# Summing expert rows at a token's rank in its group, and ending the layer group by group over gathered rows

## The chip, the cores and the metric

One core of one Trainium2 chip runs the whole program. The metric is device time in microseconds for one execution of one layer, the median of several runs. The engines are TensorE (PE in the rows, its weight load PEld), VectorE (DVE), ScalarE (ACT), GpSimd (POOL) and SyncE (SP). SP issues nearly all plain transfers in the order of its program; POOL issues those whose rows are picked by a table of indices.

## What is computed

512 tokens of 1024 features, with 16 learned tokens ahead of them, go through an attention branch and a state-space branch, which are merged and added to the input. The result `h` then goes through a mixture of experts and a last norm:

```
g_idx = argmax(v @ w_group + b_group)              # one of 4 groups
top_vals, top_idx = top_k(e_logits[g_idx], 2)      # two of the group's 8 experts
w = softmax(top_vals) * p_group[g_idx]
h = h + sum over the two experts e:  w_e * (silu(v @ gate_e) * (v @ up_e)) @ down_e
out = rmsnorm(h, norm_final)                       # v = rmsnorm(h, norm_ffn)
```

A token meets experts of one group alone. Run on its inputs, the reference's router puts 111, 155, 156 and 90 of the 512 tokens into groups 0 to 3, and no expert has more than 54 tokens.

## The kernel before

The input projections, the state-space branch and the attention come first (to about 480 us). Then `out_half` adds the merged branches to the input in `h2` (four blocks of 128 tokens on the partitions). `turn` stores each block's rows in DRAM as `vd`, and `norm_v` stores a factor behind each row. `choose`, `rank`, `find_slots` and `place` build tables with small products on TensorE and small operations on VectorE: every expert has 64 slots, experts 2p and 2p + 1 share the 128 partitions of pair p, and `idx[:, p]` and `tokf[:, p]` hold the token of each slot. `overflow` (on POOL) holds the weights of choices without a slot; a branch that runs only then is skipped here.

The expert stage runs over 16 pairs p, four of one group after another. Of a pair:

- `gather(p)` fetches the rows of the pair's tokens from `vd` into one of three buffers `xgs`, three pairs ahead, from POOL.
- `turn_x` transposes them on TensorE (`pxT`), and VectorE writes `xT`.
- `expert_gu` multiplies with the gate and up weights (`gu`), and ACT and DVE form the product `hp`.
- `expert_h` transposes that (`phT`, `hT`), `y_mm` multiplies with the down weights (`y`), and `y_split` weighs the result and splits it into two parts, `yh` on ACT and `yl` on DVE.
- `combine` adds the rows to their tokens: `st` is a matrix with a one where a slot's token number equals the column, and for each of the 4 blocks of 128 tokens and each half hh of the features two products (`yh`, `yl`) go to PSUM; DVE adds them to `h2`.

```
            for n, x in enumerate((yh_, yl_)):
                pe.matmul(pc, st[:, b * 128:(b + 1) * 128], x[:, c], start=(n == 0 and not on),
```

So a pair has 4 blocks x 2 halves x 2 parts = 16 such products. From pair 13 on (`HB`) the sums of blocks 2 and 3 stay in PSUM, which begins with eight products of `h2` with the identity (`sum_start`).

The weights stream through a ring of 6 places for gate and up weights (2 MB an expert, loaded by halves of the features, `load_gu`) and 7 for down weights (1 MB, `load_dn`). SP issues the loads of experts 2p + 6 and 2p + 7 when `expert_gu(p)` has read its places. A block `in_order` fixes the order of the named engines' instructions; elsewhere the framework's scheduler places them, also ahead of what stands earlier in the program. The last part takes the four blocks through squares, `rstd`, `scale` and a plain store of each half.

Of the kernel before, what the change touches and what calls it, by code (L numbers as in the profile page):

```python
# [9 lines left out]
F32 = mybir.dt.float32  # L10
# [9 lines left out]
T = 512  # L20
# [27 lines left out]
CAP = 64  # L48

# [10 lines left out]
for _n, _w in (("ident", 128), ("tri", 128), ("mask_s", 128), ("ones", 128),  # L60
               ("before", 128), ("ic", 104)):
    CST[_n] = (_o, _o + _w)
    _o += _w
# [8 lines left out]
def hybrid_layer(ctx: ExitStack, tc, A, out):  # L72
# [20 lines left out]
    def in_order(*engines):  # L93
        """the block's instructions run on these engines in the order of the program"""
# [51 lines left out]
    # blocks of 128 positions; block 0 starts with the meta tokens, block 4 has the last 16 positions  # L146
# [80 lines left out]
    def split_w(src, name, k, eng=dve):  # L227
        """two parts of [128, k, 1024 / k]"""
# [44 lines left out]
    def rms_feat(srcs, rngs, n, tag, nf=(0, 0)):  # L273
        """1/rms over features (partitions and list entries), broadcast over partitions"""
# [94 lines left out]
    p_misc = first[0]  # L369
# [40 lines left out]
    # dt = softplus(dt_raw + bias), token-major: column block 0 holds x chunks 0..3, block 4 the meta tokens  # L410
# [13 lines left out]
    # softplus(v) = max(v, 0) + log1p(exp(-|v|)), log1p(e) = 2 atanh(e / (2 + e))  # L424
# [13 lines left out]
    # a = dt * A;  cumulative sums within each chunk  # L438
# [14 lines left out]
    # decay[s, h] = exp(acs_last - acs_s)  # L453
# [46 lines left out]
    def gate_z(j):  # L500
        """2 silu(z)"""
# [24 lines left out]
    def ssd_a(c):  # L526
        """what a chunk needs besides the state before it"""
        n = NM if c == 4 else 128
        t0 = 0 if c == 4 else NM + c * 128
        # token-major x * dt, and times the decay to the chunk's end; B token-major, each group twice  # L530
# [3 lines left out]
        if c != 4:  # L534
            # decays between positions of the chunk: exp(acs_l - acs_s) where l >= s (elsewhere C B^T is masked)
# [127 lines left out]
    def branch_mms(pb_, wname, j, kk, oh, ol, last, parts="hl"):  # L663
        """the products of some k, first those of the weights' leading part"""
# [24 lines left out]
    # key blocks of 128 positions (block 4: 16); columns of the x queries that see each block  # L689
# [23 lines left out]
    # rows of q', k': 64 without position, 32 rotated, one that carries -max  # L713
# [13 lines left out]
    def load_wq(*which):  # L727
        """quarters of the query weights, (c, i0, i1) of each chunk c, loaded whole; what stays free of the tile"""
# [9 lines left out]
    def q_weights(c, i):  # L738
        """quarter i of chunk c of the query weights, [128, 2, 256] in two parts"""
# [9 lines left out]
    def rope(n):  # L749
        """rotated parts of the queries of heads 4 g4 .. 4 g4 + 3, in two steps"""  # L750
# [24 lines left out]
    def prep(j):  # L775
        """q' and k' of heads 2j, 2j + 1"""
# [24 lines left out]
    def find_max(h):  # L801
        """max over the keys each query sees"""
# [18 lines left out]
    def put_max(h):  # L821
        """-max into row 96 of q'"""
# [7 lines left out]
    def probs(h, h1=None):  # L830
        """exp(score - max), keys x queries, by key blocks"""
# [29 lines left out]
    def p_times_v(j, PP, eng=pool, mid=None):  # L861
        """heads 2j and 2j + 1 side by side on the array"""
# [8 lines left out]
        # the blocks' sum, for the rows' sums  # L871
# [7 lines left out]
    def row_sums(PP):  # L879
        """the rows' sums, each on 64 partitions"""  # L880
# [5 lines left out]
    def spread_sums(j, pl):  # L886
        """the sums over all partitions, 8 on each"""
# [8 lines left out]
    def invert(j, l8):  # L896
        """their inverses, each row's on 64 partitions again"""
# [46 lines left out]
    wq2[1], rotw[1] = q_weights(0, 1), q_weights(1, 1)  # L944
    PP, pos, l8s, lis = {}, {}, {}, {}
# [68 lines left out]
    # which pool holds each place of the ring, and how many of its kind lie there  # L1014
# [3 lines left out]
    def load_gu(e, parts=(0, 1)):  # L1018
        """by halves of the features"""
# [31 lines left out]
    wrt = rx.tile([128, T], F32, tag="rx", name="wrt")  # L1051
# [5 lines left out]
    # by halves of the tokens: [128, 2 blocks, 2 column tiles, 128 tokens] for two column tiles  # L1057
# [58 lines left out]
    # rows of h2 in DRAM, each with half of 1 / rms behind it  # L1116
    vd = drp.tile([T, D + 1], F32, name="vd")
# [3 lines left out]
    io32, io64, tok1 = ic[:, 4:36], ic[:, 36:100], ic[:, 100:104]  # L1121
    g_ffn = pv[:, PV["g_ffn"][0]:PV["g_ffn"][1]]
    # v @ w = (h2 @ (2 g * w)) * 1 / (2 rms(h2))
# [64 lines left out]
    def choose(b0, b1):  # L1188
# [62 lines left out]
        for b in range(nb):  # L1251
            oh12s.append(oh12[:, b])
# [522 lines left out]
```

## Time and profile before

| what | us |
|---|---|
| median of 3 runs (lowest to highest) | 850.42 (849.38 to 851.21) |
| the profiled execution: span of its instructions | 848.1 |
| what lies around the span, against the median | 2.3 |

The span runs from the first to the last instruction of the profiled execution. Times in the rows below count from its start. A row of the timeline gives start, duration, engine, line, operation and tiles, and in brackets how long the engine was idle and what ended the wait. "SPq" is SyncE's queue as it issues a transfer; the time to landing runs from the issue until all parts of the transfer have arrived.

### The profile page before, as it was taken

Reading aid. Unit: us, or ns where it says so; the run is one execution under the profiler, and the core shown is the slowest. Engines: PE = TensorE matmul, PEld = TensorE weight load, DVE = VectorE, ACT = ScalarE, POOL = GpSimd, SP = SyncE. Lnnn points to the kernel's source line nnn. Section 1 sums busy time; section 2 is a strip of 40 time slices with the busy share of each in tenths; the row PEclk is TensorE's granted clock in tenths of the full one; section 3 lists DMA queues with packets and bytes.
Section 4 is the critical chain, followed back from the end, with each engine's and each line's share of the span. In section 5 each row is a group of like instructions: output and inputs, shape, how many; then the busy total and the mean of one; then the engine's idle time right before and its main releaser. Section 6 shows DMA issues by size and latency. Waiting matters only on the chain.

```text
span 848.1 us, 11613 instructions
## 1 busy us (share of the span) xinstructions
PE 806.3 (95%) x4330; PEld 553.2 (65%) x4330; DVE 491.0 (58%) x1081; ACT 277.5 (33%) x525; POOL 133.5 (16%) x176
## 2 busy tenths in 40 slices
PE   4999999999999999999999999977999999999995
PEld 3999886777788778767665788863444444444452
DVE  4697439965357535666866654272546556556334
ACT  6445334333235552454643333210111111111114
POOL 5000104322011000024345000032000000000002
PEclk9999999999999999999999999987999999999998
DMA  7321235325212241112122955878999999999402
GB/s 246 107 90 62 100 111 163 125 85 165 75 63 100 72 164 60 35 32 61 36 74 53 388 219 213 298 276 206 419 417 420 419 418 419 418 419 412 173 1 99
DMA packets 40367, 163.53 MB, mean 193 GB/s; under 512 B 8640, under 2 KB 13008, under 8 KB 24176
## 3 DMA queue, kind: packets, MB, share of 16 engines
q1 hardware_dynamic: 36656, 156.68, 49.2%
q0 software_dynamic: 2832, 5.84, 2.3%
q8 instruction: 36, 0.59, 0.3%
q10 hardware_dynamic: 816, 0.20, 0.1%
q14 instruction: 27, 0.22, 0.1%
HBM read 159.43 MB, written 4.26 MB: 193 GB/s over the span
## 4 chain that ended last, share of the span: by engine, by line
PE 86%; DVE 5%; DMA 4%; ACT 2%; issue 1%; POOL 1%; SPq 0%; DVEq 0%; POOLq 0%; ACTq 0%
PE gu L1480 13%; PE y L1513 7%; PE pc L1542 6%; PE pbr L667 3%; PE pbr L670 3%; PE pbr L668 3%; PE po L870 2%; PE pxT L1452 2%; PE ga L240 2%; PE gs L240 2%; PE gs L241 2%; PE ga L242 2%; PE ga L241 2%; PE gs L242 2%; PE pout L1087 2%; PE pout L1089 2%
## 5 line engine op out<-in xcount | busy, mean ns | idle before, releaser
L1480 PE MATMUL gu<-gu,xT 128*64 128x512 f32 (+1 forms) x544 | 115.0, 576 | 0.0
L1480 PEld LDWEIGHTS gu<-gu,xT 128*64 128x64 f32 x544 | 37.9, 138 | 69.1 <-issue 65.5
L1545 DVE TENSOR_TENSOR h<-h,pc 128x512 f32<-128x512 f32 x108 | 66.8, 678 | 0.0
L1484 DVE SCALAR_TENSOR_TENSOR hp<-th,gu 128x256 f32<-128x256 f32 (+1 forms) x17 | 6.9, 405 | 100.0 <-ACT th L1483 100.0
L1513 PE MATMUL y<-dn,hT 128*64 128x512 f32 x256 | 58.7, 599 | 0.5 <-ACT hT L1496 0.5
L1483 ACT ACTIVATE th<-gu,rsl 128x256 f32<-128x256 f32 (+1 forms) x17 | 7.8, 461 | 149.9 <-PE gu L1480 149.9
L1542 PE MATMUL pc<-yh,st 128*128 128x512 f32 x110 | 47.3, 430 | 0.3
L816 DVE CUSTOM_DVE_ANT_0 sp<-sp,amask 128x144 f32<-128x144 f32 (+4 forms) x80 | 33.9, 459 | 18.0 <-PE sp L808 16.0
L1379 POOL DMA_INDIRECT xg<-vd,idx x16 | 16.0, 1002 | 178.4 <-PE pc L1542 161.8
L1542 PE MATMUL pc<-yl,st 128*128 128x512 f32 x110 | 43.2, 393 | 0.0
L1513 PEld LDWEIGHTS y<-dn,hT 128*64 128x64 f32 x256 | 16.9, 136 | 33.1 <-issue 26.9
L1520 ACT ACTIVATE yh<-y,wsl 128x512 fp32r<-128x512 f32 x30 | 20.6, 688 | 50.6 <-PE y L1513 50.6
L1521 DVE SCALAR_TENSOR_TENSOR yl<-y,wsl,yh 128x512 fp32r<-128x512 f32 x30 | 22.5, 751 | 20.7 <-ACT yh L1520 20.1
L1542 PEld LDWEIGHTS pc<-yh,st 128*128 128x128 f32 x110 | 20.7, 188 | 16.9 <-issue 11.4
L846 PE MATMUL st<-qs,kq 97*128 97x512 f32 (+4 forms) x80 | 28.7, 358 | 1.0 <-DVE kq L791 1.0
L1452 PEld LDWEIGHTS pxT<-cst,xg 128*128 128x128 f32 x128 | 14.4, 146 | 17.8 <-issue 17.8
L1454 DVE TENSOR_TENSOR xT<-pxT,pv 128x512 f32<-128x512 f32 x32 | 20.6, 682 | 6.6 <-PE pxT L1452 6.5
L847 PE MATMUL st<-qs,kq 97*128 97x512 f32 (+4 forms) x80 | 23.7, 296 | 0.2 <-DMA qs<-rs 0.2
L1452 PE MATMUL pxT<-cst,xg 128*128 128x128 f32 x128 | 18.3, 289 | 5.6 <-DMA xg<-vd,idx 5.6
L386 DVE SCALAR_TENSOR_TENSOR cacc<-xp,cwh,cacc 128x528 f32<-128x528 f32 x30 | 22.9, 762 | 0.4
L855 ACT ACTIVATE pw<-st 128x512 f32<-128x512 f32 (+1 forms) x32 | 16.7, 546 | 19.7 <-PE st L851 18.6
L848 PE MATMUL st<-qs,kq 97*128 97x512 f32 (+4 forms) x80 | 22.9, 294 | 0.0
(918 smaller groups left out, 2092.1 us busy)
## 6 DMA issues: line engine op xcount, KB each, us to landing
gu<-in_moe_gu_dram SPq DMA_DIRECT2D x64, 1024.0 KB, 14.7
dn<-in_moe_dn_dram SPq DMA_DIRECT2D x30, 1024.0 KB, 13.3
win<-in_win_dram SPq DMA_DIRECT2D x19, 1024.0 KB, 4.7
lm<-acd SPq DMA_DIRECT2D x16, 256.0 KB, 3.6
wbs<-in_wbs_dram SPq DMA_DIRECT2D x4, 1024.0 KB, 4.8
wba<-in_wba_dram SPq DMA_DIRECT2D x4, 1024.0 KB, 11.8
wo<-in_wout_dram SPq DMA_DIRECT2D x4, 1024.0 KB
ce<-acd SPq DMA_DIRECT2D x16, 128.0 KB, 7.3
```

Source lines behind the costliest of these rows:

```text
L240: pe.matmul(dst, ah, bh, start=(i == 0), stop=False)
L241: pe.matmul(dst, ah, bl, start=False, stop=False)
L242: pe.matmul(dst, al, bh, start=False, stop=(i == n - 1))
L667: pe.matmul(pb_, wh[:, k], oh[k], start=(k == 0), stop=False)
L668: pe.matmul(pb_, wh[:, k], ol[k], start=False, stop=False)
L816: dve.tensor_tensor_reduce(s_, s_, amask[:, L - nk + n0:L - nk + n1], 1.0, -3.0e38, op0=ALU.add, op1=ALU.max, accum_out=mx[:, n_:n_ + 1])
L846: pe.matmul(d_, kh_[0:97, kb], qh_[0:97, q0:q1], start=True, stop=False)
L1452: pe.transpose(pt[:, k * 128:(k + 1) * 128], xgs[p % NX][:, (hh * 4 + k) * 128:(hh * 4 + k + 1) * 128], ident)
L1480: pe.matmul(gu[f][r, :2 * n], xT[p][:, k, r], w, start=(k == 0), stop=(k == KD - 1), skip_group_check=True)
L1513: pe.matmul(yp[hh][e * 64:(e + 1) * 64], hT_[p][:, f, e * 64:(e + 1) * 64], dns[(2 * p + e) % ND][:, f, hh * 512:(hh + 1) * 512], start=(f ...
L1542: pe.matmul(pc, st[:, b * 128:(b + 1) * 128], x[:, c], start=(n == 0 and not on), stop=(n == 1 and (p == 15 or not kept and p < 15 - hh)), ...
L1545: dve.tensor_add(h2[:, b, c], h2[:, b, c], pc)
```

## The change

The sums of a group grow in PSUM over its four pairs, at a row that is the token's rank among its group's tokens (0 to 255, so two blocks of 128 rows and not four). `rank` now counts the 4 groups beside the 32 experts (36 columns, `ohc`), `place` puts the rank (`lpos`) beside the weight, and `y_start` compares with the rank. `group_tables`, `group_places` and `group_lists` turn the ranks into lists of tokens in pair 0. `group_rows(g)` gathers the group's rows of `h2` from `vd` into `res` in the group's third pair; `add`, `norm` and `scale` end the layer for the group in the pair behind its last, and `put_rows` scatters the finished rows to the output. `sum_start`, the 108 additions to `h2` and the last part over four blocks are gone. `vd` has 512 more rows, which begin as a copy of the input `x` and which are read only where the skipped branch has run.

The core of the diff (cut lines are marked "..."; line breaks and names as in the code):

```diff
+    vd = drp.tile([2 * T, D + 1], F32, name="vd")
+    nc.sync.dma_start(vd[T:, :D], A["x"])
+    nc.sync.dma_start(vd[T:, D:], A["x"][:, :1])
     PP, pos, l8s, lis = {}, {}, {}, {}
...
         dve.tensor_tensor(pen, bc(ic[:, None, 0:4], 4), bc(gf, 4), op=ALU.not_equal)
+        pool.tensor_scalar(ohc[:, b0:b1, 32:], pen, -1.0, 1.0, op0=ALU.mult, op1=ALU.add)
...
-                pe.matmul(rk[:, b * 32:(b + 1) * 32], trib if b2 == b else onesb, oh12s[b2],
+                pe.matmul(rk[:, b * 36:(b + 1) * 36], trib if b2 == b else onesb, oh12s[b2],
                           start=(b2 == 0), stop=(b2 == b), skip_group_check=True)
+        act.activation(rkg[:, b0:b1], ranks(b0, b1)[:, :, 32:], AF.Copy)
+        for k in range(2):
+            pool.tensor_tensor(vw[:, :, k, 1].rearrange("p b (g e) -> p b g e", g=4),
+                               ak[:, :, k].rearrange("p b (g e) -> p b g e", g=4),
+                               rkg[:, b0:b1, :, None].to_broadcast([128, b1 - b0, 4, 8]), op=ALU.mult)
...
     def overflow(b0):
+        pool.tensor_tensor(g4_, ohc[:, b0:b1, 32:], rkg[:, b0:b1], op=ALU.mult)
+        pool.tensor_tensor(g4_[:, :, :2], g4_[:, :, :2], g4_[:, :, 2:], op=ALU.add)
+        pool.tensor_tensor(gk[:, b0:b1], g4_[:, :, 0], g4_[:, :, 1], op=ALU.add)
         pool.tensor_scalar(wx, rkk, CAP - 0.5, None, op0=ALU.is_gt)
+        pool.tensor_scalar(g4_[:, :, 2], gk[:, b0:b1], GCAP - 0.5, None, op0=ALU.is_gt)
+        pool.tensor_tensor(wx, wx, g4_[:, :, 2:3].to_broadcast([128, b1 - b0, 2]), op=ALU.add)
+        pool.tensor_scalar(wx, wx, 0.5, None, op0=ALU.is_gt)
...
+    fin = btile("fin", n=T, tag="v").rearrange("p k n -> p (k n)")
+    res, gfin = [fin[:, b * (D + 1):(b + 1) * (D + 1)] for b in range(2)], fin[:, 2 * D + 2:3 * D + 2]
...
+        for x in res:
+            pool.memset(x, 0.0)
...
+    nc.sync.dma_start(gfin, bcast_row(A["g_fin"], D))
+
+    def put_rows(places, rows):
+        nc.gpsimd.indirect_dma_start(out=out, out_offset=bass.IndirectOffsetOnAxis(ap=places, axis=0),
+                                     in_=rows, in_offset=None, bounds_check=T - 1, oob_is_err=False)
...
-            if p == HB[0] and kh:
-                sum_start(HB[1])
...
-        dve.tensor_scalar(st, iot, tokf[:, p:p + 1], None, op0=ALU.is_equal)
+        dve.tensor_scalar(st, iot, lpos[:, p:p + 1], None, op0=ALU.is_equal)
...
-    def combine(p, hh, blocks=range(4)):
+    def combine(p, hh, blocks=range(2)):
         st, yh_, yl_ = y_[p]
...
+            if p % 4 == 0:
+                sums[b, hh] = ps("pc")
             for n, x in enumerate((yh_, yl_)):
+                pe.matmul(sums[b, hh], st[:, b * 128:(b + 1) * 128], x[:, c], start=(n == 0 and p % 4 == 0),
+                          stop=(n == 1 and p % 4 == 3), skip_group_check=True)
-            if not kept and p < 15 - hh:
-                dve.tensor_add(h2[:, b, c], h2[:, b, c], pc)
...
+    def group_places():
+        for h in range(2):
+            for b in range(4):
+                pe.matmul(pg[:, h], rrg[:, b, h * 128:(h + 1) * 128], gtab[:, b], start=(b == 0), stop=(b == 3),
+                          skip_group_check=True)
...
+    def group_rows(g):
+        for b in range(2):
+            nc.gpsimd.indirect_dma_start(out=res[b], out_offset=None, in_=vd,
+                                         in_offset=bass.IndirectOffsetOnAxis(ap=gsrc[:, b, g:g + 1], axis=0),
+                                         bounds_check=2 * T - 1, oob_is_err=False)
...
+    def add(b, hh):
+        r = res[b][:, cols(hh)]
+        dve.tensor_add(r, r, sums[b, hh])
+        act.activation(sums[b, hh], r, AF.Square, scale=D ** -0.5, accum_out=fq[:, 2 * b + hh:2 * b + hh + 1])
+
+    def norm(b):
+        r = fq[:, 8 + b:9 + b]
+        dve.scalar_tensor_tensor(r, fq[:, 2 * b:2 * b + 1], EPS, fq[:, 2 * b + 1:2 * b + 2], op0=ALU.add, op1=ALU.add)
+        pool.tensor_tensor(r, r, mhalf[:, :1], op=ALU.pow)
+
+    def scale(g, b):
+        x = res[b][:, :D]
+        dve.scalar_tensor_tensor(x, x, fq[:, 8 + b:9 + b], gfin, op0=ALU.mult, op1=ALU.mult)
+        put_rows(gdst[:, b, g:g + 1], x)
...
-    with in_order(dve, pe, nc.sync):
+    with in_order(act, dve, pe, pool, nc.sync):
...
                 if p:
-                    combine(p - 1, 1, range(CB))
+                    combine(p - 1, 1, (0,))
                 expert_h(p)
+                if p == 0:
+                    group_places()
                 if p:
-                    combine(p - 1, 1, range(CB, 4))
+                    combine(p - 1, 1, (1,))
...
-                nc.sync.dma_start(dns[25 % ND][:, 0], bcast_row(A["g_fin"], D))
...
+            if last and p < 15:
+                for b in range(2):
+                    add(b, 0)
+            if p and p % 4 == 0:
+                for b in range(2):
+                    norm(b)
+                for b in range(2):
+                    scale(g - 1, b)
+            if p % 4 == 2:
+                group_rows(g)
+        for hh in range(2):
+            for b in range(2):
+                combine(15, hh, (b,))
+                add(b, hh)
+                if hh:
+                    norm(b)
+        for b in range(2):
+            scale(3, b)
```

Three places show what the diff alone does not. The first is SP's queue at the start of the program, before the change. `win` are chunks of the input projection's weights, `xm` the last 16 positions of the input and the last `xin` its fourth block.

```order
L224 DMA win_169<-in_win_dram 128x2048
L224 DMA win_376<-in_win_dram 128x2048
L159 DMA xm_96<-in_x_dram 16x512
L159 DMA xm_97<-in_x_dram 16x512
L156 DMA xin<-in_x_dram 128x1024
L349 DMA pv<-in_pv_dram 128x86
```

The same place after the change:

```order
L225 DMA win_169<-in_win_dram 128x2048
L225 DMA win_376<-in_win_dram 128x2048
L948 DMA vd<-in_x_dram 512x1024
L949 DMA vd<-in_x_dram 512x1
L160 DMA xm_96<-in_x_dram 16x512
L160 DMA xm_97<-in_x_dram 16x512
L157 DMA xin<-in_x_dram 128x1024
L350 DMA pv<-in_pv_dram 128x86
```

The two copies into `vd`, written down behind the query weights of the attention, have moved to the head of the queue, ahead of `xm` and the fourth block of the input.

The second place is POOL from the routing tables of the last block to the first gathers of the expert stage, before the change (`wrest` ends one block of `overflow`):

```order
L1302 TENSOR_SCALAR ru<-ru 128x2 [waits DVE_49]
L1303 TENSOR_TENSOR ru<-ru 128x2 [waits Pool_49]
L1304 TENSOR_TENSOR ru<-ru 128x64 [waits Pool_49]
L1305 TENSOR_TENSOR wrest<-ru 128x32 [waits Pool_49]
L1379 DMA xg_5299<-vd,idx 128x1025 [waits DMAHW4_49,DMAHW3_49,DMAHW5_49,DMAHW2_49,DMAHW6_49,DMAHW1_49,DMAHW7_49,DMAHW0_49,DVE_49]
L1379 DMA xg_5300<-vd,idx 128x1025
```

After the change, from the last block's two products with the rank (`rkg`) on:

```order
L1289 TENSOR_TENSOR ru<-ru,rkg 128x32 [waits DMAHW3_49,DMAHW0_49,DMAHW5_49,DVE_49,Activation_49]
L1289 TENSOR_TENSOR ru<-ru,rkg 128x32
L1321 TENSOR_TENSOR ru<-ohc,rkg 128x4
L1330 TENSOR_TENSOR wrest<-ru 128x32 [waits Pool_49]
L1324 TENSOR_SCALAR ru<-ru 128x2 [waits DVE_49]
L1322 TENSOR_TENSOR ru<-ru 128x2 [waits Pool_49]
L1323 TENSOR_TENSOR gk<-ru 128x1 [waits Pool_49]
L1325 TENSOR_SCALAR ru<-gk 128x1 [waits Pool_49]
L1326 TENSOR_TENSOR ru<-ru 128x2 [waits Pool_49]
L1327 TENSOR_SCALAR ru<-ru 128x2 [waits Pool_49]
L1410 DMA xg_5339<-vd,idx 128x1025 [waits DMAHW4_49,DMAHW3_49,DMAHW5_49,DMAHW2_49,DMAHW6_49,DMAHW1_49,DMAHW7_49,DMAHW0_49,DVE_49]
L1410 DMA xg_5340<-vd,idx 128x1025
```

Between the clearing of the three `xgs` and the first gather POOL had 13 operations and now has 35, ten of them behind the last block's rank.

The third place is the end of POOL's program after the change: the last group's gathers, its two powers and its two scatters. Before, these stores were eight plain ones from SP.

```order
L1621 DMA fin<-vd,gsrc 128x1025 [waits Activation_49]
L1621 DMA fin<-vd,gsrc 128x1025 [waits DMASW5_49,DMASW3_49,Activation_49]
L1636 TENSOR_TENSOR fq<-fq,mhalf 128x1 [waits DVE_49] x2
L1426 DMA out_dram<-fin,gdst 512x1024 [waits DMASW6_49,DMASW4_49,DVE_49]
L1426 DMA out_dram<-fin,gdst 512x1024 [waits DMASW6_49,DMASW5_49,DVE_49]
```

Transfers from POOL signal their landing on eight semaphores in turn, and the first scatter signals on DMASW6: the second scatter waits for the landing of the first, since both write the output.

## Rows read from the trace of the kernel before

**Rows 1.** The chain in order of time over one pair: start, us, engine, line.

```profile
658.57 7.02 PE gu L1480 x32
665.59 1.02 PE pxT L1452 x8
666.61 0.93 PE pc L1542 x4
667.53 0.22 PE phT L1494 x2
667.75 0.92 PE pc L1542 x4
668.67 3.58 PE y L1513 x16
672.26 2.04 PE pc L1542 x8
```

**Rows 2.** Windows: busy us by engine, granted clock, DMA share, GB/s.

```profile
579.00:586.00 7.00, 7.00 (x28) 2.25 (x30) 0.84 (x3) 0.00 (x0) 0.99 (x1) 0.81 0.62 43
586.00:790.00 204.00, 202.93 (x951) 91.23 (x948) 113.32 (x217) 29.04 (x52) 11.87 (x12) 1.00 1.01 418
```

**Rows 3.** DMA issues: engine, number, KB each, median us to landing.

```profile
gu<-in_moe_gu_dram SPq DMA_DIRECT2D x64, 1024.0 KB, 14.7
dn<-in_moe_dn_dram SPq DMA_DIRECT2D x30, 1024.0 KB, 13.3
...
xg<-vd,idx POOLq DMA_INDIRECT x16, 8.5
```

**Rows 4.** Line 1032, SP, 700 to 800 us: issues of the gate and up weights.

```profile
L1032 SPq DMA_DIRECT2D gu<-in_moe_gu_dram x20: 327/330/386, 709.4 to 776.2; - x20
...
DMA to landing us min/median/max: 14.5/14.9/16.4
```

**Rows 5.** The chain in order of time, from pair 13 to the end.

```profile
788.09 3.63 PE pcl L1532 x8
...
820.56 7.06 PE gu L1480 x64
...
830.08 2.73 PE y L1513 x12
```

**Rows 6.** Timeline of ACT at the start: fourth block's squares, second weight split.

```profile
17.22 1.04 ACT L184 ACTIVATE junk<-xin 128x1024 bf16<-128x1024 f32 x1
...
19.48 1.04 ACT L233 ACTIVATE win1h<-win 128x1024 fp32r<-128x1024 f32 x1
```

**Rows 7.** Timeline of PE at the start: the second column tile.

```profile
22.38 0.84 PE L320 MATMUL first1a<-uh,win1h 128*128 128x256 f32 x5
```

**Rows 8.** Timeline of POOL ahead of the expert stage.

```profile
561.16 2.73 POOL L1371 MEMSET xg<- 128x1025 f32 x3 [3.75 <-PE rk L1278]
...
568.73 0.38 POOL L1302 TENSOR_SCALAR ru<-ru 128x2 f32<-128x2 f32 x1 [1.72 <-DVE ovi L1349]
...
572.42 1.17 POOL L1379 DMA_INDIRECT xg<-vd,idx  x1 [2.33 <-DMA dn<-in_moe_dn_dram]
```

**Rows 9.** Timeline of PE: the first transposes of the expert stage.

```profile
576.98 1.94 PE L1452 MATMUL pxT<-cst,xg 128*128 128x128 f32 x8 [5.57 <-DMA xg<-vd,idx]
```

**Rows 10.** Groups by line: shapes, number, busy us, mean ns, idle before.

```profile
L1545 DVE TENSOR_TENSOR h<-h,pc 128x512 f32<-128x512 f32 x108 | 66.8, 678 | 0.0
...
L1521 DVE SCALAR_TENSOR_TENSOR yl<-y,wsl,yh 128x512 fp32r<-128x512 f32 x30 | 22.5, 751 | 20.7 <-ACT yh L1520 20.1
...
L1609 ACT ACTIVATE gu<-pcl 128x512 f32<-128x512 f32 x4 | 2.4, 596 | 0.9 <-PE pcl L1542 0.9
...
L1626 DVE SCALAR_TENSOR_TENSOR gu<-pcl,fq,dn 128x512 f32<-128x512 f32 x3 | 2.1, 742 | 0.0
...
L1609 ACT ACTIVATION_READ_ACCUMULATOR gu<-pcl 128x1 f32 x4 | 0.8, 200 | 0.0
```

**Rows 11.** The output's stores: issues of line 1631, and time to landing.

```profile
L1631 SPq DMA_DIRECT2D out_dram<-gu x8: 332/332/349, 838.4 to 844.6; - x8
...
DMA to landing us min/median/max: 2.0/2.0/2.0
```

More of the change, by code (lines that the diff above doesn't have):

```diff
@@ L48 @@
 CAP = 64
+GCAP = 256
 PV = {}
@@ L60 @@
 for _n, _w in (("ident", 128), ("tri", 128), ("mask_s", 128), ("ones", 128),
-               ("before", 128), ("ic", 104)):
+               ("before", 128), ("ic", 109)):
     CST[_n] = (_o, _o + _w)
@@ L1522, in y_split @@
                                  op0=ALU.mult, op1=ALU.subtract)
-    HB = (13, (2, 3))
-    hs, more = {}, {}
-    def sum_start(blocks):
+    sums = {}
+    def combine(p, hh, blocks=range(2)):
+        st, yh_, yl_ = y_[p]
+        c = cols(hh)
         for b in blocks:
-            for hh in range(2):
-                hs[b, hh] = ps("pcl")
-                pe.matmul(hs[b, hh], ident, h2[:, b, hh * 512:(hh + 1) * 512], start=True, stop=False, skip_group_check=True)
-    def combine(p, hh, blocks=range(4)):
-        st, yh_, yl_ = y_[p]
-        c = slice(hh * 512, (hh + 1) * 512)
-        for b in blocks:
-            kept = (b, hh) in hs
-            on = kept or p == 15 and hh
-            pc = hs[b, hh] if kept else more[b, hh] if on else ps("pc")
-            for n, x in enumerate((yh_, yl_)):
-                pe.matmul(pc, st[:, b * 128:(b + 1) * 128], x[:, c], start=(n == 0 and not on),
-                          stop=(n == 1 and (p == 15 or not kept and p < 15 - hh)), skip_group_check=True)
-            if not kept and p < 15 - hh:
-                dve.tensor_add(h2[:, b, c], h2[:, b, c], pc)
-            elif not kept:
-                more[b, hh] = pc
+            if p % 4 == 0:
+                sums[b, hh] = ps("pc")
+            for n, x in enumerate((yh_, yl_)):
+                pe.matmul(sums[b, hh], st[:, b * 128:(b + 1) * 128], x[:, c], start=(n == 0 and p % 4 == 0),
+                          stop=(n == 1 and p % 4 == 3), skip_group_check=True)
@@ L1554, in hybrid_layer @@
         for p in range(16):
+            g, last = p // 4, p % 4 == 3
             expert_gu(p)
@@ L1574, in hybrid_layer @@
                 expert_h(p, (0,))
-                combine(p - 1, 1, (2, 3))
+                combine(p - 1, 1, (0,))
                 y_mm(p, 0, 0)
@@ L1581, in hybrid_layer @@
                     y_split(p, hh)
-                combine(p - 1, 1, (0, 1))
+                combine(p - 1, 1, (1,))
             for e in range(2 * p + ND, min(2 * p + ND + 2, 30)):
@@ L1600, in cols @@
-    def cols(hh):
-        return slice(hh * 512, (hh + 1) * 512)
-    def summed(b, hh):
-        return hs[b, hh] if (b, hh) in hs else h2[:, b, cols(hh)]
-    def squares(b, hh):
-        if b > 1 and (b, hh) not in hs:
-            add(b, hh)
-        act.activation(junk[:, b, cols(hh)], summed(b, hh), AF.Square, scale=D ** -0.5, accum_out=fq[:, 2 * b + hh:2 * b + hh + 1])
-    def rstd(b):
-        r = fq[:, 8 + b:9 + b]
-        dve.scalar_tensor_tensor(r, fq[:, 2 * b:2 * b + 1], EPS, fq[:, 2 * b + 1:2 * b + 2], op0=ALU.add, op1=ALU.add)
-        pool.tensor_tensor(r, r, mhalf[:, :1], op=ALU.pow)
@@ L1616, in add @@
-    def add(b, hh):
-        dve.tensor_add(h2[:, b, cols(hh)], h2[:, b, cols(hh)], more[b, hh])
-    def gain(eng, b, hh):
-        eng.tensor_tensor(obs[:, b, cols(hh)], summed(b, hh), gfin[:, cols(hh)], op=ALU.mult)
-    def scale(b, hh, by):
-        o, r = obs[:, b, cols(hh)], fq[:, 8 + b:9 + b]
-        if by is dve:
-            dve.scalar_tensor_tensor(o, summed(b, hh), r, gfin[:, cols(hh)], op0=ALU.mult, op1=ALU.mult)
-        else:
-            act.activation(o, summed(b, hh) if by is pool else o, AF.Copy, scale=r)
-            if by is pool:
-                pool.tensor_tensor(o, o, gfin[:, cols(hh)], op=ALU.mult)
-        nc.sync.dma_start(out[b * 128:(b + 1) * 128, cols(hh)], o)
@@ L1663 @@
+            if p and p % 4 == 0:
+                for b in range(2):
[12 more added lines that the diff above has]
+            scale(3, b)
 PAIRED = np.arange(32).reshape(2, 16).T.ravel()
```

127 lines of the change are left out of this document (72 added, 55 removed).

## The prediction

> **What bounds the kernel now.** I read four views in this order. First the chain of what ended last, in order of time: over the expert stage it is TensorE alone, pair after pair, with no idle piece between its groups. [rows 1] is one period: 7.02 for `gu`, 1.02 for the transposes, 0.93 + 0.92 + 2.04 for the 16 products of `combine` (3.89), 0.22, and 3.58 for `y`, together 15.73 us. Then the windows: from 586 to 790 TensorE is busy for 202.93 of 204.00 us at granted clock 1.00, but the DMA engines show a share of 1.01 at 418 GB/s [rows 2]. So two things are full at once. The third view, the transfers, says how full: each pair needs four loads of `gu` and two of `dn` of 1 MB each [rows 3], 6.29 MB, and some 64 gathered rows (1024 choices over 16 pairs) of 4,100 bytes, 0.26 MB; 6.55 MB at 418 GB/s are 15.7 us. The reader is to see that the two periods are equal: TensorE can't go much faster without waiting for weights.
>
> The fourth view is the margin. The loads of `gu` land 14.9 us after their issue (14.5 to 16.4 over the last hundred microseconds, so the backlog does not grow), and the last is issued at 776.2 [rows 4]: it lands at 791.1. It is the second expert's second half, used halfway through the last `gu`, which runs from 820.56 for 7.06 us [rows 5], so from 824.1. The stream of weights is **33.0 us ahead** of its use. That lead is what TensorE can gain before the stream sets the end.
>
> **What TensorE loses of its work.** Eight of the 16 products go: half of 3.89, 1.95 us a pair. Ahead of the end of the last `gu` (820.56 + 7.06 = 827.6) lie 14 whole `combine`s and the first half of pair 14's, 14 x 1.95 + 0.98 = 28.3, and `sum_start`, 3.63 [rows 5]: **-31.9**. The 108 additions of 0.678 us on DVE [rows 10] go too, but DVE is busy for 91 of 204 us [rows 2] and ends no wait of the chain; they are costed at nothing. If the two products of a half and block had been held up by them, the gain would be larger; the unbroken row of TensorE says they are not. Added on TensorE: the tables of places in pair 0, some 16 small products and four columns more in the ranks, about 1.0; and the places in PSUM that stay occupied for four pairs, for which I allow one short wait of 0.15 a pair, as an estimate between nothing and the 0.34 of a small hand-over: **+3.2**. Without the start's terms the last `gu` would end at 827.6 - 31.9 + 3.2 = 798.9 if nothing else held it.
>
> **The start.** The two copies of `x` into `vd` (2.1 MB) now stand on SP ahead of `xm` and the input's fourth block. No row has such a copy. At 418 GB/s it takes 5.0 us, and 512 pieces of four bytes a little (0.3); below it could be nearly hidden, above it may go at half that rate since it reads and writes DRAM, with up to 2 us for the pieces: 12. I take 5.3, because it shares the engines with loads that run at the stream's rate. The fourth block had landed no later than 17.22, when ACT squares it; from there ACT works without a gap to the second weight split, 19.48 to 20.52 [rows 6], and TensorE takes that at 22.38 [rows 7]: a slack of 1.86. ACT works in order, so 17.0 + 5.3 = 22.3, plus 3.3 of ACT's work (17.22 to 20.52), is 25.6 in place of 22.38: +3.2. TensorE then waits some 3 us, after which I allow 1.0 for work at the lower clock (waiting costs that elsewhere: [rows 9], below). **+4.2**, with bounds 1.5 and 9.
>
> **POOL ahead of the first gather.** 35 operations in place of 13. Four small ones took from 568.73 to 570.09, where the wait of 2.33 ahead of 572.42 begins [rows 8]: 0.34 each. What ends that wait by the profile is a load of `dn`, with which the gather has nothing to do; the other named ones are the rows of `vd`. 35 x 0.34 = 11.9 behind the memset's end at 563.89 is 575.8 against 572.42, +3.4. The 22 added ones are partly spread over earlier blocks: **+3.0**, bounds 0 (all covered by waits) and 4.5. TensorE waits for this gather alone (5.57 ahead of 576.98, [rows 9]), and the loads behind it on SP wait for TensorE to free the ring: the whole stream moves with it.
>
> **What is added to the stream.** Groups 0 to 2 hold 422 tokens: gathered 1.73 MB, scattered 1.73 MB, and about half of the last group's 90 rows ahead of the last load, 0.18 MB: 3.64 MB, at 418 GB/s **+8.7 us**. Indices out of range are skipped, so no full 256 rows. Bounds: 0, if the backlog had room (the share of 1.01 excludes it), and twice that, if a scattered row costs double.
>
> So the stream's last load lands at 791.1 + 4.2 + 3.0 + 8.7 = **807.0**; the second half of `gu` follows, 3.5, and it ends at E = 810.5. TensorE's own work would end at 798.9 + 7.2 = 806.1. The stream is 4.4 us later: TensorE gains 28.7 and the stream slips 8.7, together 37.4 against a lead of 33.0. In the last pairs TensorE must wait for weights.
>
> **The tail behind E.** Before, 827.6 to the span's end at 848.1: 20.5. Now: the end of `y` was 830.08 + 2.73 = 832.8 [rows 5], 5.2 behind E; one pair of products less lies on that path (0.46): E + 4.7. Splitting takes about 0.7 on ACT and 0.75 on DVE, two products 0.5, four additions 4 x 0.68, the last square 0.60 + 0.20, two small operations of the norm with their hand-overs about 1.5, and the scale of 1,024 columns, twice 0.742 [rows 10]: E + 13.2 for the first scatter. A plain store of the output lands in 2.0 (the last one issued at 844.6, [rows 11]); a gather took 572.42 to 576.98, 4.5, in an almost idle stretch, and 8.5 as the median [rows 3, 8, 9]. I take 4.5 for a scatter, the row that is nearest: rows picked by an index and no queue ahead. The second scatter waits on POOL for the first one's landing; nothing else is behind it. E + 13.2 + 4.5 + 4.5 + 1.5 (844.6 + 2.0 to 848.1) = **E + 23.7**, 3.2 more than before, with bounds 18.7 and 31.7.
>
> Sum: 810.5 + 23.7 = 834.2 for the span. The profiled execution's span of 848.1 lies 2.3 under the median of 850.4; with that, **836.5 us**, 13.9 less than before.
>
> **Rivals.** *TensorE stays the bound.* If the added rows slip into the stream without delaying it (4.4 of the 8.7 us would do), E is 806.1 and the time 806.1 + 23.7 + 2.3 = 832.1. For it speaks that the lead of 33 us is only just used up, against it the share of 1.01. The Trainium skill (DMA: Bandwidth & Descriptors, Specifications) gives 435 GB/s as the fabric's ceiling, so that an estimate by that page has 4% of room left; the trace shows 418 at a full share, and I hold to it. Chance 0.20.
>
> *The waits slow the clock.* In the bound case TensorE waits some 2 us a pair, in pieces, in the last few pairs. Behind the wait of 5.57 the transposes took 1.94 in place of 1.02 [rows 9, 1]: the lower of its two levels, and over 579 to 586 the granted clock is 0.81 [rows 2]. If what follows the last load ran so, half of `gu`, a pair of products and `y` (3.5 + 0.5 + 2.73) would take twice as long, 6.7 more: about 843. Against it: from 586 on the clock is 1.00. The Trainium skill (TensorE: Matmul & The Clock Gate, HAM oscillation) warns that waiting for transfers between bursts of products throttles the engine again and again; in this trace the one wait that shows it is that of 5.57, and no row has a train of short ones. Chance 0.13.
>
> *The indirect transfers stall the weights: slower.* From 579 to 586, while the first gathers run, the engines show a share of 0.62 at 43 GB/s: 7 us that carry what 0.7 would at 418 [rows 2], 6.3 us lost. The change puts seven pairs of indirect transfers into the stream; if three stall it so, the time is 836.5 + 18.9 = 855.4. It is slower than before from 13.9 / 6.3 = 2.2 stalls on. Against it: most of the 16 gathers of `xg` [rows 3] lie between 586 and 790, where the rate is 418; for it, that no indirect store lies in any row. Chance 0.07.
>
> **How the numbers follow.** The forecast has 0.60, and its own range, from the bounds of the start, POOL and the tail taken together, is 830 to 842. The other cases lie at 832, 843 and 855; the range **829 to 845** leaves out the stalls and some extremes. 0.2% (1.7 us) is about what a measurement here can tell from no change. Faster: 0.60 + 0.20 + 0.13 less a little for a mixture of the upper bounds, **0.91**; the same 0.02; slower 0.07.
>
> **What would show it.** Right: the wait ahead of `gu` ends on a load of `gu` in the last pairs, the share stays about 1.01 to near 807, the period of earlier pairs is near 14 us, `first1a` starts near 25.6, the first gather near 579.6 (572.42 + 7.2), and the second scatter starts when the first has landed. Wrong: no wait for weights up to the end (then 832), a rate well under 418 around the scatters, a granted clock under 1.00 in the last pairs, or a copy of `x` that takes 10 us and more.

## The result, and the profile after

| what | before | changed |
|---|---|---|
| median, us (lowest to highest) | 849.95 (849.38 to 851.21) | 841.83 (840.23 to 844.10) |
| ratio, 95% interval | | 0.9912 (0.9891 to 0.9933) |
| the same kernel in a second set of runs | 849.65 | 839.32; 0.9879 (0.9863 to 0.9895) |
| the profiled execution: span | 848.1 | 842.3; in the second set 838.0 |

The kernel before has four runs here, one more than in the table ahead of the prediction. The change is 8 to 10 us faster, where 13.9 were forecast; the range held the time. The span of 842.3 belongs to the slowest of the four runs, so each comparison below says which profile it takes.

The chain of waits of the changed kernel, in order of time (start, us, engine, line), at the beginning and at the end of the expert stage:

```profile
584.38 4.43 DMA xg<-vd,idx
588.95 1.94 PE pxT L1503 x8
590.89 9.16 PE gu L1529 x32
...
604.65 5.28 PE y L1562 x16
...
611.06 7.07 PE gu L1529 x32
...
812.55 7.06 PE gu L1529 x64
...
831.98 4.31 DMA out_dram<-fin,gdst
```

Three pieces make up the difference of the two profiled executions. The first transposes stand at 588.95 where they stood at 576.98 [rows 9]: **+12.0**. From there to the end of the last `gu` it takes 819.61 - 588.95 = 230.7 where it took 827.62 - 576.98 = 250.6 [rows 5, 9]: **-20.0**. From the end of that `gu` to the end of the span it takes 22.7 where it took 20.5: **+2.2**. Together -5.8, as the spans say. In the second profile of the same kernel the first piece is +8.5 (585.44), and the two others are the same to a microsecond.

**One pair.** The same chain over a pair in the middle of the stage, to be held against [rows 1]:

```profile
740.62 7.07 PE gu L1529 x32
747.76 0.48 ACT th L1532
748.26 0.43 DVE hp L1533
748.72 0.43 DVE hp L1534
749.28 0.42 PE phT L1543 x2
749.79 0.39 ACT hT L1545
750.23 3.65 PE y L1562 x16
753.88 1.12 PE pc L1583 x4
755.00 7.07 PE gu L1529 x32
```

What the reader is to see: before, every row of the pair was TensorE's. Now between `gu` and `y` the chain runs over ACT and DVE (`th`, two steps of `hp`, `phT`, `hT`), 2.5 us from 747.69 to 750.23. TensorE has work beside it for some 2.2 only (transposes 1.02, two products on either side of `phT` 0.47 each, `phT` itself 0.22 as in [rows 1]); before it had 3.09, and the chain was hidden. So a pair takes 14.38, not 15.73 - 1.95 = 13.78. Of these 0.6 us the uncovered chain is 0.4. The other 0.2 lie in `gu`, `y` and `pc`, which take 0.05 to 0.10 longer each than in [rows 1] (for `pc` half of 2.04); why was not looked into.

**The stream.** Windows (busy us by engine, granted clock, DMA share, GB/s), for [rows 2], and the issues of the gate and up weights, for [rows 4]:

```profile
590.00:600.00 10.00, 10.00 (x38) 3.21 (x37) 1.57 (x4) 0.00 (x0) 1.75 (x4) 0.75 0.45 54
600.00:800.00 200.00, 194.15 (x906) 76.19 (x908) 73.37 (x162) 39.24 (x80) 33.56 (x30) 0.99 1.02 419
...
L1037 SPq DMA_DIRECT2D gu<-in_moe_gu_dram x64: 327/328/1372, 475.0 to 791.3; - x64
```

From 600 to 800 the share is full again (1.02, 419 GB/s), and TensorE idles for 5.9 of 200 us. Its waits in that stretch name `hp` and the tables of pair 0 and no load (its weight load names one of `dn`, twice, for 0.6 us together). The last load of `gu` is issued at 791.3 (before 776.2). In the changed kernel's relatives below such a load lands some 21 us after its issue, so near 812 by estimate; it is used from 816.1. By that the lead of 33.0 us has shrunk to about 4.

**The start and the end.** Timelines of the changed kernel: ACT and TensorE where the fourth block of the input arrives (for [rows 6, 7]), then POOL at the first gather (for [rows 8]) and at the last two scatters. Behind them a window while the copy runs, then the last two copies of `vbT` on DVE, from which the last routing tables start, before the change and after it.

```profile
23.84 0.63 ACT L188 ACTIVATE junk<-xm 16x512 bf16<-16x512 f32 x1 [8.06 <-DMA xm<-in_x_dram]
...
25.22 1.04 ACT L185 ACTIVATE junk<-xin 128x1024 bf16<-128x1024 f32 x1
...
27.48 1.04 ACT L234 ACTIVATE win1h<-win 128x1024 fp32r<-128x1024 f32 x1
...
28.63 2.05 PE L321 MATMUL first1a<-uh,win1h 128*128 128x256 f32 x8
...
584.38 1.19 POOL L1410 DMA_INDIRECT xg<-vd,idx  x1 [0.92 <-DVE lpos L1384]
...
831.98 2.07 POOL L1426 DMA_INDIRECT out_dram<-fin,gdst  x1 [0.18 <-issue]
837.12 0.98 POOL L1426 DMA_INDIRECT out_dram<-fin,gdst  x1 [3.07 <-DMA out_dram<-fin,gdst]
```

```profile
16.00:24.00 8.00, 5.31 (x24) 5.02 (x24) 1.03 (x1) 0.17 (x1) 1.18 (x3) 1.00 1.05 256
```

```profile
562.51 0.75 DVE L1155 COPY vbT<-pvT 128x256 f32<-128x256 f32 x2
```

```profile
573.78 0.74 DVE L1161 COPY vbT<-pvT 128x256 f32<-128x256 f32 x2
```

ACT stands idle for 8.06 us until `xm` arrives, and only then squares it and the fourth block: 25.22 in place of 17.22, and `first1a` follows at 28.63 in place of 22.38. From 16 to 24 us the DMA engines are full (share 1.05) but move 256 GB/s, where the prediction counted the copy at 418. By the trace's records of single packets the pieces of four bytes take some 0.3 us of that, so it is the copy of the 2 MB. The first gather is held for 0.92 by a table that DVE writes (`lpos`), not by POOL's own operations, which end at 583.47. From the copies of `vbT` to the first gather it takes 10.60 where it took 9.91 [rows 8], 0.7 longer. The second scatter starts when the first has landed.

### The profile page after: what moved, and what is told of

It is laid out like the page before. It is cut to its first block, busy times and chain, and to the rows that moved or that the text cites. A ratio compares the mean times of both kernels' runs of the same rounds, so it can differ in the third digit from the quotient of the medians.

```text
span 842.3 us, 11392 instructions
## 1 busy us (share of the span) xinstructions
PE 783.6 (93%) x4202; PEld 531.0 (63%) x4202; DVE 441.7 (52%) x1005; ACT 281.9 (33%) x541; POOL 162.6 (19%) x222
## 4 chain that ended last, share of the span: by engine, by line
PE 81%; DMA 6%; DVE 6%; ACT 4%; issue 2%; POOL 0%; POOLq 0%; ACTq 0%; SPq 0%; DVEq 0%
PE gu L1529 14%; PE y L1562 7%; PE pbr L671 3%; PE pbr L669 3%; PE pbr L668 3%; PE po L871 2%; DMA xm<-in_x_dram 2%; PE pc L1583 2%; PE ga L241 2%; PE gs L241 2%; PE ga L243 2%; PE ga L242 2%; PE gs L242 2%; PE pout L1092 2%; PE gs L243 2%
## 5 line engine op out<-in xcount | busy, mean ns | idle before, releaser
L1562 PE MATMUL y<-dn,hT 128*64 128x512 f32 x256 | 60.4, 614 | 0.9
L1583 PE MATMUL pc<-yh,st 128*128 128x512 f32 x60 | 27.7, 462 | 0.0
L301 POOL TENSOR_TENSOR rfs<-rfm,mhalf 128x4 f32<-128x4 f32 (+1 forms) x5 | 7.6, 1519 | 92.6 <-DVE rfm L300 92.6
L877 POOL TENSOR_TENSOR pw<-pw 128x400 f32<-128x400 f32 x14 | 15.9, 1157 | 44.4 <-PE po L871 44.4
L1583 PE MATMUL pc<-yl,st 128*128 128x512 f32 x60 | 23.7, 396 | 0.0
```

The source lines that it names most:

```text
L1562: pe.matmul(yp[hh][e * 64:(e + 1) * 64], hT_[p][:, f, e * 64:(e + 1) * 64], dns[(2 * p + e) % ND][:, f, hh * 512:(hh + 1) * 512], start=(f ...
L1583: pe.matmul(sums[b, hh], st[:, b * 128:(b + 1) * 128], x[:, c], start=(n == 0 and p % 4 == 0), stop=(n == 1 and p % 4 == 3), skip_group_ch ...
```

## The experiments

Twelve kernels ran, in three sets, each with five rounds beside the kernel before. Ratios are against the kernel before of the same set; 0.001 is 0.85 us.

**The copy of `x` out of the head of SP's queue.**

```diff
-    nc.sync.dma_start(vd[T:, :D], A["x"])
-    nc.sync.dma_start(vd[T:, D:], A["x"][:, :1])
+    with tc.issue_after(loads["wukv"].ins):
+        nc.sync.dma_start(vd[T:, :D], A["x"])
+        nc.sync.dma_start(vd[T:, D:], A["x"][:, :1])
```

> The two copies of x into vd stand behind the load of wukv (near 277 us of the trace) and no longer at the head of SP's queue; all else is as in the changed kernel. In the trace of the change TensorE's rows stand 7.7 us later than before from 25 us on, 9.3 later from 150 on, 11.3 later from 470 on. Theory A, only the copy's own delay goes: 841.8 - 7.7 = 834.1. Theory B, the later steps of 1.6 and 2.0 are consequences of the late start too: 841.8 - 11.3 = 830.5. Rival, the stream of weights of the expert stage sets the end whatever the start does: the stream starts with the first product of the stage and so moves with it, so this rival forecasts the same and is not told apart here; a gain under 5 would mean that something else holds the start.

Measured: 830.84 (one of the five runs at 835.38, the others within 1.3 us), ratio 0.9792 (0.9770 to 0.9814), span 829.0. TensorE's timeline at the start and at the expert stage:

```profile
21.87 1.19 PE L321 MATMUL first1a<-uh,win1h 128*128 128x256 f32 x8
...
576.65 1.94 PE L1504 MATMUL pxT<-cst,xg 128*128 128x128 f32 x8 [5.06 <-DMA xg<-vd,idx]
```

The time is Theory B's: the first transposes are back at 576.65, a little ahead of the 576.98 before. So the late start was the copy's, but for the 0.7 us from `vbT` to the first gather, which are here too (561.60 to 572.20). That the later steps are consequences of the copy alone is not shown: they differ between executions of one kernel (12.0 and 8.5 above), and the last kernel below, whose copy stands late, has one of 1.1 us as well (at 472.57 ACT has waited 3.50 for a load, where the kernel before has waited 2.44 at 472.31). Against the changed kernel's two ratios the copy's place is worth 7.4 to 10.2 us (0.0087 to 0.0120).

**The same copy added to the kernel before**, alone (with `vd` doubled, and `gather` reading its first half).

```diff
-    vd = drp.tile([T, D + 1], F32, name="vd")
+    vd = drp.tile([2 * T, D + 1], F32, name="vd")
+    nc.sync.dma_start(vd[T:, :D], A["x"])
+    nc.sync.dma_start(vd[T:, D:], A["x"][:, :1])
```

> The kernel before, with the copies of x into a second half of vd added and nothing else of the change; they stand at the head of SP's queue, behind the same two loads as in the change. Theory A, the copies' delay at the start goes through to the end whatever the rest is: 7.7 more at 25 us, and with the later steps 9 to 12 more, 859 to 862. Rival B, the lead of the stream or a later wait takes up part of it: under 5 more, below 855.

Measured: 858.42, ratio 1.0106 (1.0090 to 1.0122), 7.6 to 10.4 us slower: close to Theory A, just under its figures. TensorE's timeline:

```profile
28.11 2.06 PE L320 MATMUL first1a<-uh,win1h 128*128 128x256 f32 x8
```

It stood at 22.38 [rows 7]. In this execution the delay stays at 7.1 to 7.6 us up to the end (855.1 - 848.1 = 7.0); in most of the others with the copy at the head another 1.5 came at 150 us, and in some up to 2 more at 470 us. What decides on these later steps was not looked into.

**The tables of the groups ahead of the first transposes.**

```diff
+        group_tables()
+        group_places()
+        group_lists()
         for hh in range(2):
             turn_x(0, hh)
...
-                if p == 0:
-                    group_tables()
...
-                if p == 0:
-                    group_places()
...
-            if p == 0:
-                group_lists()
```

> The tables of the groups' rows (four comparisons and the tables on DVE, eight small products on TensorE, the lists) stand ahead of the first transposes, in the wait of 5.2 us for the first gathered rows, and no longer between the products of pair 0. In the change's trace pair 0, from its first product of gu to that of pair 1, takes 20.2 us where it took 16.7. Theory A, TensorE's own row of work sets the end: 3.3 less, 838.5. Rival B, the stream of weights is right behind: its last loads are issued at 791.3 and land close to 814, so the last gu can't end before about 817.5 where it ends at 819.6: 2.1 less, 839.7. Rival C, the tables delay the first gathers or transposes: no gain, 841.8 or more.

Measured: 842.71, ratio 0.9920 (0.9905 to 0.9934): rival C. Its chain and DVE's timeline:

```profile
584.58 4.80 another core or an unknown queue
...
591.45 1.81 PE pxT L1503 x8
593.26 8.95 PE gu L1529 x32
609.50 7.07 PE gu L1529 x32
...
589.66 1.14 DVE L1598 TENSOR_SCALAR rrg<-iot,gk 128x256 bf16<-128x256 f32 x4 [8.34 <-DMA wrt<-in_wr_dram]
```

Pair 0 itself falls from 20.2 to 16.2 us, as it should, but the comparisons on DVE wait for 8.34 us and hold the transposes. The transfer named had landed long before, so it was another; the likeliest is the third gather, issued at 584.54, since the chain has the wait run from 584.58 and end 4.80 later, which was not settled. What the tables cost in pair 0 is thereby shown, 3.9 us (20.17 against 16.24), and no gain from moving them: the stage from the first transposes on is shorter by 3 to 4 us, but it starts later.

**The products of `combine` moved, to cover the chain behind `gu`.** First form:

```diff
                 if p:
-                    combine(p - 1, 1, (0,))
+                    combine(p - 1, 0)
+                    if (p - 1) % 4 == 3:
+                        for b in range(2):
+                            add(b, 0)
                 expert_h(p)
...
                 if p:
-                    combine(p - 1, 1, (1,))
+                    combine(p - 1, 1)
...
-            if p < 15:
+            if p == 14:
                 combine(p, 0)
-            if last and p < 15:
-                for b in range(2):
-                    add(b, 0)
```

> All eight products of combine of a pair stand in the next pair, four ahead of the transposes of hp and four between them and y, in place of two, two and four behind y. In the change's trace a pair takes 14.40 us where half of the 16 products less would give 13.78: the chain th, hp, phT, hT, 2.6 us behind gu, has too little work of TensorE beside it. Theory A, that chain alone lengthens the pair: the period falls to about 13.75, 14 pairs by 0.6 are 8.5 less, 833.3. Theory B, the stream of weights is right behind TensorE and takes over: the last gu ends near 817.5 in place of 819.6, 2.1 less, 839.7, and TensorE shows waits for loads of gu in the last pairs. Rival C, the period does not fall, since PSUM or the split results hold it: 841.8.

Measured: 840.14, ratio 0.9891 (0.9872 to 0.9910). The time is Theory B's, but the trace is not: TensorE's waits (total, times, longest) show

```profile
PE y L1562 <- ACT hT L1545: 6.2, 3, 2.1
```

and no load. The beginnings of two pairs in the chain, and one of the three waits on TensorE's timeline:

```profile
736.52 6.87 PE gu L1529 x32
...
750.08 6.87 PE gu L1529 x32
...
717.62 5.35 PE L1562 MATMUL y<-dn,hT 128*64 128x512 f32 x16 [2.06 <-ACT hT L1545]
```

Pairs took 13.56 us: with all eight products beside it the chain behind `gu` is covered again, and the pair is even a little shorter than the 13.78 counted. But the squares of a group's end, which I had put ahead of `hT` on ACT, cost 3.85 us behind each of three groups: a wait of 2.1, and `y` at 5.35 in place of 3.58 (granted clock 0.57 from 718 to 722). The edit had made a wait of its own, and the run tells nothing of the stream. The second form puts these additions behind the splits of `y`:

```diff
                     y_split(p, hh)
                     if p and p % 4 == 0:
+                        add(hh, 0)
                         add(hh, 1)
```

> As the first kernel with the products of combine moved into the next pair, but the additions of a group's end stand behind the splits of y in the next pair. In the first one pairs took 13.56 us, except that behind each group's last pair TensorE waited 2.1 us for hT, since ACT had two squares of the group's end to do first, and the pair took 3.85 longer. Theory A, TensorE's row of work alone sets the end: 13 pairs of 13.56 in place of 14.40 are 11 us less than the change, 830.8. Theory B, the stream of weights is right behind: the last loads of gu, issued near 788 and landing some 21 us later, hold the last gu, whose second half can't start before 809 to 811, so that it ends near 813 in place of the 816.3 of the first kernel: 837 to 838, with waits of TensorE for loads of gu in the last pairs. Rival C, another hand-over at the group's end takes the place of hT: pairs behind a group stay over 15 us.

Measured: 840.16, ratio 0.9880 (0.9865 to 0.9895), the changed kernel's own 0.9879. Waits of TensorE and of its weight load from 600 to 812 (total, times, longest), TensorE's longest one on its timeline, the window, and the times from issue to landing of the loads of `gu` from 700 on:

```profile
PE gu L1529 <- DMA gu<-in_moe_gu_dram: 4.5, 4, 1.5
...
PEld gu L1529 <- DMA gu<-in_moe_gu_dram: 9.5, 7, 2.4
...
751.25 3.65 PE L1529 MATMUL gu<-gu,xT 128*64 128x512 f32 x14 [1.48 <-DMA gu<-in_moe_gu_dram]
...
600.00:800.00 200.00, 191.99 (x909) 80.30 (x910) 74.12 (x162) 38.44 (x79) 34.57 (x31) 0.99 1.02 419
...
DMA to landing us min/median/max: 19.8/21.9/22.9
```

Theory B, and even the 2 to 4 us that it left are gone: now TensorE waits for weights, as soon as its own work is as short as the prediction took it to be. From the first transposes (587.98) to the start of the last `gu` it takes 222.3 us here, in the changed kernel's two profiles 223.5 and 222.7. TensorE itself stands idle for a load for at most 1.5 us at a time (the 2.4 are its weight load's), and behind pair 0 the granted clock is 1.00 in every stretch of 2 us up to 806. The Trainium skill (TensorE: Matmul & The Clock Gate, HAM oscillation) warns that transfers waited for between bursts throttle the engine; these waits did not. Waits of 2.1 us for `hT` in the first form and of 2.2 for the tables in pair 0 did, as the rows of `y` at 5.35 and 5.28 show.

**The stores of groups 0 to 2 left out**, in that kernel and in the changed one.

```diff
-        put_rows(gdst[:, b, g:g + 1], x)
+        if g == 3:
+            put_rows(gdst[:, b, g:g + 1], x)
```

> The kernel of this call with the products moved, and the rows of groups 0 to 2 are not stored (left out: six of eight scatters, 1.73 MB). Theory B, the stream of weights sets the end: 1.73 MB at 418 GB/s are 4.1 us, and the time falls by 2 to 4 against that kernel, until TensorE's own row sets the end. Theory A, TensorE's row alone: within 1 us of that kernel. Rival C, POOL's waits ahead of its scatters hold the later gathers and so TensorE: a fall of more than 5.

> The changed kernel without the stores of groups 0 to 2 (left out: six of eight scatters, 1.73 MB). The same cut took 4.2 off the kernel whose products were moved. Theory A, TensorE's row of work, with the chain behind gu too little covered, sets the end of the changed kernel: within 1 us of the changed kernel. Theory B, the stream sets its end as well: 2 to 4 less.

Measured: with the products moved 835.98, ratio 0.9833 (0.9820 to 0.9846), 4.2 us under that kernel's 840.16, near the 4.1 us of 1.73 MB at 418 GB/s (in the two profiled executions 3.4 between the first transposes and the last `gu`, 0.6 behind it, 1.2 ahead, which are chance). TensorE still waits for loads there. In the changed kernel 839.24, ratio 0.9889 (0.9872 to 0.9906), beside 839.32: nothing, Theory A. So the stream sets the end of the one and not of the other. TensorE's own row of work sets the changed kernel's end, with the stream just behind it.

**The changed kernel once more**, in the same set as the last kernel and the one without the very last scatter below.

> The changed kernel once more, beside the other kernels of this call: 840 to 843, as before; its first transposes between 586 and 589, its pairs 14.40 apart, no wait of TensorE for a load of gu.

Measured: 839.32, as in the table above, and first transposes at 585.44, both a little under what was expected; pairs 14.40 apart, no wait for a load of `gu`.

**The last part.** First the order, block 0 sent off before block 1 is added up:

```diff
                 if hh:
                     norm(b)
-        for b in range(2):
-            scale(3, b)
+                    scale(3, b)
```

> In the last part the block 0 of the last group is normed, scaled and sent off before block 1 gets its last addition. In the change's trace the first scatter is issued at 831.98, the second starts at 837.1 when the first has landed, and the end is at 842.3. Theory A, the landing of one scatter behind the other sets the end: the first goes off 1.3 earlier, 840.5. Rival B, block 1's work or the second scatter's own issue sets the end: no change, 841.8.

Then the changed kernel without the very last scatter:

```diff
-        put_rows(gdst[:, b, g:g + 1], x)
+        if (g, b) != (3, 1):
+            put_rows(gdst[:, b, g:g + 1], x)
```

> The changed kernel without the very last scatter, that of ranks 128 to 255 of the last group, which has 90 tokens, so that it stores nothing here (left out only for groups of more than 128). Theory A, the second scatter's wait for the first one's landing and its own landing lie on the path: the trace ends at 842.3, where the first has landed at 836.3: 4 to 5.5 less, 836.5 to 838. Rival B, the program's end waits for something else: no change.

Measured: 837.44, ratio 0.9864 (0.9844 to 0.9885), and 836.02, ratio 0.9844 (0.9830 to 0.9859). The timelines of POOL at the end, of the first and of the second kernel:

```profile
827.39 1.05 POOL L1426 DMA_INDIRECT out_dram<-fin,gdst  x1 [1.61 <-DVE fin L1640]
...
831.53 1.03 POOL L1426 DMA_INDIRECT out_dram<-fin,gdst  x1 [2.23 <-DMA out_dram<-fin,gdst]
```

```profile
828.52 2.07 POOL L1426 DMA_INDIRECT out_dram<-fin,gdst  x1 [0.18 <-issue]
```

From the end of the last `gu` (816.10 and 816.16) to the end of the span it takes 20.7 and 19.1 in place of 22.7. The new order is worth 2.0 us by that and 1.3 by the ratios (against the changed kernel's second set, 0.9879), in line with the 1.3 expected, though the intervals of these ratios overlap. The second scatter costs 3.6 by the spans and 3.3 by the medians, less than the 4 to 5.5 expected; that the end waits for the first one's landing in any case would explain it, and was not tested. It stores no row here.

**Together.** The copy late and the new order of the last part, then these two with the moved products (second form).

> The copies of x late and the order of the last part changed, both as tried by themselves (830.8 and 837.4 against 841.8). Theory A, the two lie one behind the other on the path: 841.8 - 11.0 - 4.4 = 826.4. Theory B, some 2 us of the second gain were a start that happened to be earlier (its first transposes stood at 586.6 against 588.95), which the late copy gives anyway: 828.5.

> The three together: copies late, last part reordered, products moved (with the additions behind the splits). Theory A, TensorE's row alone: 11 less than the kernel with the first two, 815 to 818. Theory B, the stream of weights right behind: 2 to 4 less, 823 to 825.

Measured: 829.71, ratio 0.9768 (0.9750 to 0.9786), and 829.65, ratio 0.9762 (0.9748 to 0.9775). Both beat the changed kernel by some 10 us and the kernel before by 20. The first lies near Theory B, 1.2 over it; the second misses both theories, for the moved products add nothing to the time. The first transposes and the last `gu`, in the first kernel and in the second, and the second one's waits for loads from 600 to 812 (the first has none for `gu`):

```profile
576.22 1.94 PE L1504 MATMUL pxT<-cst,xg 128*128 128x128 f32 x8 [4.96 <-DMA xg<-vd,idx]
...
798.60 7.13 PE L1530 MATMUL gu<-gu,xT 128*64 128x256 f32 x64
```

```profile
577.87 1.94 PE L1504 MATMUL pxT<-cst,xg 128*128 128x128 f32 x8 [5.12 <-DMA xg<-vd,idx]
...
798.67 7.13 PE L1530 MATMUL gu<-gu,xT 128*64 128x256 f32 x64
...
PEld gu L1530 <- DMA gu<-in_moe_gu_dram: 7.6, 6, 2.2
...
PE gu L1530 <- DMA gu<-in_moe_gu_dram: 3.2, 4, 1.4
```

The last `gu` starts at the same time in both, but the second one's stage began 1.65 later in this execution: from the first transposes on it takes 220.8 in place of 222.4. So the moved products gain 1.6 us there and then wait for loads: two limits, TensorE's row with its uncovered chain and the stream of weights, lie within some 2 us of one another.

## Why the prediction was right or wrong

- **The start, +4.2: the mechanism right, the size short.** The direct delay is 6.3 to 7.7 us, and the first transposes stand 8.5 to 12.0 later. The copy was counted at 418 GB/s, 5.3 us; at the 256 GB/s of its window its 2.1 MB are some 8 us by estimate, within the bounds given. The sum also let ACT start on the fourth block as soon as it is there, at 22.3, and forgot what ACT has to do ahead of it: `xm` is behind the copy as well and arrives near 23.8, and its squares take 1.4 us. That later steps add to a delay was not in the sum at all.
- **POOL, +3.0: too much, 0.7.** The gather waits for a table on DVE (0.92 us for `lpos`), and POOL's added operations fit in ahead of that.
- **TensorE, -31.9 + 3.2: the step that failed.** The 1.95 a pair and `sum_start` went as counted. But the four products that left the place between `gu` and `y` had been the cover of the chain `th`, `hp`, `phT`, `hT`; I counted them as work on the path and nothing else, and allowed 0.15 a pair for waits for places in PSUM, which none of TensorE's waits names. It is 0.6: some 8 us in 13 pairs, and with the products put back beside the chain a pair took 13.56. The tables in pair 0 cost 3.9 in place of 1.0, since TensorE waits 2.2 us for DVE and then runs `y` for 5.28 in place of 3.65 at the lower clock (0.50 from 606 to 608). With both, -31.9 + 8 + 3.9 is the measured -20.
- **What is added to the stream, +8.7: right as far as seen.** With the true start the last load is due at 791.1 + 12.0 + 8.7 = 811.8; issued at 791.3 and, by estimate, 21 us on its way it lands near 812. The 1.73 MB of six scatters cost 4.2 us where the stream sets the end.
- **The forecast, the stream becomes the bound: only where TensorE is made as fast as forecast.** In the changed kernel the rival that TensorE stays the bound holds, to which I gave 0.20, but at a longer pair: the sign of being wrong, no wait for weights up to the end, came, but not the 832 that went with it. That the range held the time is in part luck, since what the uncovered chain costs is in none of its terms. The other two did not come: the granted clock stays at 0.99, and the rate at 419 GB/s with all indirect transfers in it.
- **The last part, E + 23.7: nearly right,** E + 22.7. The first scatter at E + 12.4 (13.2 forecast), its landing 4.31 (4.5), the second's wait as described.
- **The total** came out 3 to 5 us above 836.5. By the first profile the start with POOL took 4.8 more than the 7.2 forecast (by the second 1.3) and the stage from the first transposes to E 4.3 more (3.5), while the tail took 1.0 less; POOL's 3.0, of which 2.3 did not come, hid part of the short start.

## What to carry to other kernels

Work taken off the bounding engine is not only time saved: ask which latency it covered, and add up that chain against what is left beside it. A transfer without dependencies that a scheduler may place at the head of a queue holds up all that stands behind it there, though nothing waits for the transfer itself; one line that ties it to a later load was worth about as much here as the change itself (7.4 to 10.2 us against 8 to 10). When two resources are full at once, a gain on one is worth no more than the lead of the other, and the proof is to shorten each by itself.

## What was not expected of the hardware

A scatter whose rows are all out of range still holds the end for some 3.4 us. An indirect store in a quiet stretch lands after 3.3 to 4.3 us, a plain one in 2.0 [rows 11]. A copy from DRAM to DRAM filled the DMA engines at 256 GB/s, where loads fill them at 418. In the expert stage waits of TensorE of 2.1 and 2.2 us were followed by the lower clock, waits of up to 1.5 us for loads were not. And the added row transfers, all with indices, left the total rate where it was: 419 GB/s from 600 to 800 with them, 419 without six of the scatters.
